# A quarter of the modulation sums of a two-layer diffusion block: product on GpSimd, row sum on ScalarE, bias on VectorE

## The chip, the core and the metric

The kernel runs on one core of a Trainium2 chip. A core has five engines that each run their own instruction stream in order and wait for one another through semaphores: TensorE (PE, matrix products into PSUM; PEld is its weight load), VectorE (DVE), ScalarE (ACT), GpSimd (POOL) and SyncE (SP, which here only issues loads). The metric is the device time of one launch in microseconds (us), lower is better. Times of single stages come from one execution taken by the hardware profiler.

## The reference, cut to what matters

Two layers of a transformer block work on 256 latent tokens and 256 context tokens of width 1024. Every sublayer (feedforward, mixer, feedforward) is normalised, scaled and shifted, and gated by a modulation vector that comes from a condition: `c` for the latent tokens and `c_ctx` for the context tokens.

```
mod = (jax.nn.silu(c) @ mod_w[i] + mod_b[i]).reshape(bsz, 3, 3, 1, D_MODEL)
modc = (jax.nn.silu(c_ctx) @ mod_w[i] + mod_b[i]).reshape(3, 3, D_MODEL)
...
lat = lat + 0.5 * mod[:, 0, 2] * _swiglu(_modulate(lat, norm_g[i, 0], mod[:, 0, 0], mod[:, 0, 1]), ffn_w13[i, 0], ffn_w2[i, 0])
```

`mod_w[i]` is 1024 x 9216 in float32. Its product with two vectors is the part that the change touches; nearly all other work is in the large products of feedforward, convolution and attention.

## The kernel before, in words

Activations lie transposed in SBUF: 8 tiles `x[:, m, :]` of 128 features by 512 tokens (256 latent, 256 context). Each float32 product is made of three products of float32r halves: a weight or activation is split in a high half `wh` (ScalarE, L107, a copy with rounding) and a low half `wl` (VectorE, L108, the difference), and `mm3` (L132) issues wh x mh, wh x ml and wl x mh (L136, L137, L138).

A feedforward (`ffn`, L813) goes in three thirds of the 22 hidden blocks. In each third, `Pair` objects (L696) compute gate and up projections with a Strassen-like scheme of seven products of quarter matrices: `head` (A11, A12), `five` (S1), `six` (S2, S4), `seven` (S3) and `four` (A22). A pair loads two raw tiles; GpSimd negates one half (L709) and then issues an accumulating load (L712) and another for A22's low half (L114), and VectorE forms the sums S (L731, L739). After `seven` VectorE adds (L776), reading the PSUM tile `p`, into which `four` adds its product afterwards. Then come gm = silu(gate) x up (L785) and its split into gh (ScalarE) and gl (VectorE), which the following `project` (L588) uses as its last operand tiles. `project` works on 8 output tiles; with a pair still open, its first three output tiles run interleaved with that pair's `seven` and `four`, and their last operand comes at the end. Outputs are scaled by the gate column (L563, ScalarE) and added to x by an accumulating DMA that GpSimd issues (L566), or by VectorE (L572).

The modulation of layer 0's first two chunks is made on TensorE at the start. All the rest is made as small **units** that fill VectorE: `jobs` lists tiles of 128 x 1024 weights (`modT`), one per output column tile (`kt = 2 * pair + j`, with j = 0 or 1). SyncE loads one job ahead into the ring of raw tiles `wr` (8 buffers, shared with the weights, L102) or, late in the kernel, into `wm` (L167). One unit (`mod_unit`, L171) multiplies the raw tile with the row `scbc[:, v, :]` (silu of the condition, the same in all partitions), sums along the row, scales, adds the bias and writes one column `mt[:, kt, v]`: one fused VectorE instruction over 128 x 1024 elements (L177) with a small read of the accumulator behind it. There are two units per job, v = 0 for the latent and v = 1 for the context condition; from layer 1's chunk 5 on only v = 0. `tick(n)` (L214) is called by the loops and issues n units: about one per pair (0.9), and three to four per output tile in the first five tiles of `project` (L624, L635). `mod_ready` and `gate` issue what is still missing when a column is needed.

Outside of stretches written out by hand, a scheduler sets the order on each engine from these program positions, so instructions of one engine can change places when the program changes.

Of the kernel before, what the change touches and what calls it, by code (L numbers as in the profile page):

```python
# [12 lines left out]
AF = mybir.ActivationFunctionType  # L13
ALU = mybir.AluOpType
# [34 lines left out]
def hybrid_kernel(ctx: ExitStack, tc: tile.TileContext, a: dict, out: bass.AP):  # L49
    nc = tc.nc  # L50
# [12 lines left out]
    def nm(s):  # L63
        uid[0] += 1
        return f"{s}{uid[0]}"
# [14 lines left out]
    ccol, modb, normg, ident, rowsum = (first[:, a:b] for a, b in zip(CUTS, CUTS[1:]))  # L80
    ccol = ccol.rearrange("p (k v) -> p k v", v=2)
    modb = modb.rearrange("p (l c) -> p l c", l=2)
    normg = normg.rearrange("p (l j k) -> p l j k", l=2, j=3)
    x = act.tile([P, KT, T2], F32, name="x", tag="x")
    for q in range(4):
# [7 lines left out]
        out=const.tile([P, 1], F32, name="silu", tag="silu"), in_=eps_t, func=AF.Silu  # L93
# [4 lines left out]
    scbc = mp.tile([P, 2, D], F32, name="scbc", tag="scbc", bufs=1)  # L98


    def load_raw(src, n=1024):
        raw = wp.tile([P, 1024], F32, name=nm("wr"), tag="wr", bufs=8)  # L102
        nc.sync.dma_start(raw[:, :n], src)
        return raw
# [47 lines left out]
    done = {}  # L152

    def mod_tile(l, ch):
        if (l, ch) not in modv:
            modv[l, ch] = const.tile([P, KT, 2], F32, name=f"mod{l}_{ch}", tag=f"mod{l}_{ch}")
            done[l, ch] = 0
        return modv[l, ch]
# [12 lines left out]
    def mod_unit(l, ch, pair, raw, j, v):  # L171

        mt = mod_tile(l, ch)
        kt = pair * 2 + j
        col = ch * KT + kt
        junk = mp.tile([P, D], BF16, name=nm("junk"), tag="junk", bufs=1)
        nc.vector.tensor_tensor_reduce(  # L177
            out=junk,
            in0=raw,
            in1=scbc[:, v, :],  # L180
            scale=0.5 if ch in (2, 8) else 1.0,
            scalar=modb[:, l, col : col + 1],
            op0=ALU.mult,
            op1=ALU.add,
            accum_out=mt[:, kt, v : v + 1],
        )
        done[l, ch] += 1
# [12 lines left out]
    def next_unit():  # L200
        if not units:
            l, ch, pair, j = jobs.pop(0)
            mod_tile(l, ch)
            raw = coming.pop() if coming else load_mod(l, ch, pair, j)
            if jobs:
                coming.append(load_mod(*jobs[0]))
            units.extend((l, ch, pair, raw, j, v) for v in range(streams(l, ch)))
        if place:
            with tc.issue_after(place[0]):
                mod_unit(*units.pop(0))  # L210
        else:
            mod_unit(*units.pop(0))
# [1177 lines left out]
    for kv in range(KVH):  # L1390
# [7 lines left out]
        out=scq, in0=rq[:, :16], scalar1=float(P) ** -0.5, scalar2=None, op0=ALU.mult  # L1398
# [76 lines left out]
    for i in range(2):  # L1475
        raw = [load_raw(a["wo"][i, :, c : c + 1024]) for c in (0, 1024)]
# [133 lines left out]
```

## Time and profile before

| | |
|---|---|
| median of 3 runs | 1549.41 us (1548.96 to 1549.91) |
| the profiled execution's own time | 1548.97 us |
| its span, first to last instruction | 1547.2 us |
| TensorE busy | 1533.5 us (99%) |
| VectorE busy | 1298.2 us (84%) |
| ScalarE busy | 852.2 us (55%) |
| GpSimd busy | 301.3 us (19%) |
| modulation units (L177) | 224, 269.9 + 19.2 us |

Line numbers such as L177 are those of the kernel before. In a row of a group, `out<-in` names the tiles, then come the shapes, the count, the busy time in us, the mean of one in ns, and after the second bar the idle time of the engine just before, with what ended it. A row of the timeline begins with its start in us from the span's start and its duration; brackets at its end hold the idle time before it and what ended that. In the list of waits, "A <- B" is A waiting for B.

### The profile page before, as it was taken

What the parts mean: (1) busy time and instruction counts of PE and PEld (TensorE: products, weight loads), DVE (VectorE), ACT (ScalarE), POOL (GpSimd) and SP (SyncE); (2) the same over time, 40 slices, a digit from 0 to 9 for tenths busy, and PEclk for the clock granted to TensorE, in tenths of its full rate; (3) what the DMA queues carried; (4) which work ended last, traced back from release to release, by engine and by line L of the source; (5) the groups of instructions that cost most, each with busy time, mean ns of one, the idle gap of its engine ahead of it and who ended that gap; (6) DMA issues with size and microseconds to landing.
All of it is one profiled execution on the core that took longest, in us unless ns stands there. A gap on an engine that the chain in (4) does not pass through costs nothing.

```text
span 1547.2 us, 27333 instructions
## 1 busy us (share of the span) xinstructions
PE 1533.5 (99%) x10594; PEld 1423.6 (92%) x10594; DVE 1298.2 (84%) x1964; ACT 852.2 (55%) x1468; POOL 301.3 (19%) x265
## 2 busy tenths in 40 slices
PE   8999999999999999999999999999999999999999
PEld 6898998999999899989999899989999899998888
DVE  5888788898989999968979889958968788998676
ACT  5644554645655376446456466446456456774553
POOL 0013313402231023042052112043042002300000
PEclk9999999999999999999999999999999999999999
DMA  9568768765356636695796625785697743476562
GB/s 377 199 188 235 162 184 232 164 194 143 75 143 175 206 91 151 212 216 135 213 214 153 207 68 136 220 189 138 210 220 182 253 159 114 142 246 220 170 195 76
DMA packets 97474, 278.80 MB, mean 180 GB/s; under 512 B 11456, under 2 KB 13120, under 8 KB 97344
## 3 DMA queue, kind: packets, MB, share of 16 engines
q1 hardware_dynamic: 69408, 228.10, 45.4%
q0 software_dynamic: 25920, 47.20, 18.1%
q10 hardware_dynamic: 2016, 1.76, 0.4%
q8 instruction: 83, 1.36, 0.4%
q14 instruction: 47, 0.39, 0.1%
HBM read 262.07 MB, written 1.05 MB: 170 GB/s over the span
## 4 chain that ended last, share of the span: by engine, by line
PE 89%; DVE 6%; DMA 2%; ACT 1%; issue 1%; POOL 0%; SPq 0%; DVEq 0%; POOLq 0%; ACTq 0%
PE p L138 8%; PE p L137 8%; PE p L136 8%; PE py L137 8%; PE py L136 8%; PE py L138 8%; PE q L138 6%; PE q L136 6%; PE q L137 6%; PE py L144 2%; PE pu L144 2%; PE pg L144 2%; DVE wl L108 1%; DMA wr<-in_w 1%; PE py L146 1%
## 5 line engine op out<-in xcount | busy, mean ns | idle before, releaser
L107 ACT ACTIVATE wh<-wr 128x1024 fp32r<-128x1024 f32 (+2 forms) x454 | 400.5, 909 | 289.2 <-PE py L137 94.5
L108 DVE TENSOR_TENSOR wl<-wr,wh 128x1024 fp32r<-128x1024 f32 (+2 forms) x454 | 468.6, 1056 | 107.0 <-ACT wh L107 87.0
L177 DVE CUSTOM_DVE_ANT_0 junk<-wr,scbc,first 128x1024 bf16<-128x1024 f32 x209 | 269.9, 1291 | 2.2 <-DMA wr<-in_modT 0.2
L137 PE MATMUL py<-gl,wh 128*128 128x512 f32 (+1 forms) x570 | 213.4, 374 | 0.0
L136 PE MATMUL py<-gh,wh 128*128 128x512 f32 (+1 forms) x570 | 213.4, 374 | 0.0
L138 PE MATMUL py<-gh,wl 128*128 128x512 f32 (+1 forms) x570 | 212.8, 373 | 0.0
L709 POOL TENSOR_SCALAR wr<-wr 128x512 f32<-128x512 f32 x66 | 125.4, 1900 | 424.0 <-DMA wr<-in_w 162.7
L136 PE MATMUL p<-th,wh 128*128 128x256 f32 x528 | 149.5, 283 | 0.0
L138 PE MATMUL p<-th,wl 128*128 128x256 f32 x528 | 149.4, 283 | 0.0
L137 PE MATMUL p<-tl,wh 128*128 128x256 f32 x528 | 149.4, 283 | 0.0
L138 PEld LDWEIGHTS py<-gh,wl 128*128 128x128 f32 x570 | 107.3, 188 | 19.1
L136 PEld LDWEIGHTS py<-gh,wh 128*128 128x128 f32 x570 | 107.4, 188 | 18.3
L137 PEld LDWEIGHTS py<-gl,wh 128*128 128x128 f32 x570 | 107.4, 188 | 18.2
L138 PE MATMUL q<-bh,wl 128*128 128x256 f32 x400 | 113.2, 283 | 0.0
L137 PE MATMUL q<-bl,wh 128*128 128x256 f32 x400 | 113.2, 283 | 0.0
L136 PE MATMUL q<-bh,wh 128*128 128x256 f32 x400 | 113.2, 283 | 0.0
L136 PEld LDWEIGHTS p<-th,wh 128*128 128x128 f32 x528 | 101.3, 192 | 0.4
L137 PEld LDWEIGHTS p<-tl,wh 128*128 128x128 f32 x528 | 101.3, 192 | 0.4
L138 PEld LDWEIGHTS p<-th,wl 128*128 128x128 f32 x528 | 101.3, 192 | 0.0
L114 POOL DMA_DIRECT2D w4l<-in_w x56 | 53.2, 949 | 229.9 <-ACT w4l L113 183.5
L566 POOL DMA_DIRECT2D x<-yg x48 | 44.7, 995 | 215.7 <-ACT yg L563 172.4
L772 ACT ACTIVATE sg<-sg 128x512 f32<-128x512 f32 x56 | 35.3, 631 | 89.0 <-DVE sg L768 88.9
(321 smaller groups left out, 4199.4 us busy)
## 6 DMA issues: line engine op xcount, KB each, us to landing
wr<-in_w SPq DMA_DIRECT2D x120, 512.0 KB, 4.8
wr<-in_modT SPq DMA_DIRECT2D x113, 512.0 KB, 5.1
wr<-in_w2b SPq DMA_DIRECT2D x64, 448.0 KB, 4.0
wr<-in_w2a SPq DMA_DIRECT2D x32, 512.0 KB, 4.4
wr<-in_w SPq DMA_DIRECT2D x56, 256.0 KB, 4.6
wr<-in_w POOLq DMA_DIRECT2D x56, 256.0 KB, 6.0
w4l<-in_w POOLq DMA_DIRECT2D x56, 256.0 KB, 5.8
x<-yg POOLq DMA_DIRECT2D x48, 256.0 KB, 7.6
```

The costliest lines, as they stand in the source:

```text
L107: nc.scalar.activation(out=hi, in_=src, func=AF.Copy)
L108: return nc.vector.tensor_tensor(out=lo, in0=src, in1=hi.bitcast(F32), op=ALU.subtract)
L114: nc.gpsimd.dma_start(out=lo, in_=src, accum_op=ALU.add)
L136: nc.tensor.matmul(ps, wh, mh, start=first, stop=False, **kw)
L137: nc.tensor.matmul(ps, wh, ml, start=False, stop=False, **kw)
L138: return nc.tensor.matmul(ps, wl, mh, start=False, stop=last, **kw).ins
L144: nc.tensor.matmul(ps, w[0], m[2], start=first and n == 0, stop=False)
L146: nc.tensor.matmul(ps[:, :S], w[1], m[0], start=False, stop=last and n == len(ms) - 1)
L177: nc.vector.tensor_tensor_reduce(out=junk, in0=raw, in1=scbc[:, v, :], scale=0.5 if ch in (2, 8) else 1.0, scalar=modb[:, l, col : col + 1 ...
L566: nc.gpsimd.dma_start(out=x[:, m, :], in_=t, accum_op=ALU.add)
L709: nc.gpsimd.tensor_scalar(out=r1[:, :T2], in0=r2[:, :T2], scalar1=-1.0, scalar2=None, op0=ALU.mult)
L772: nc.scalar.activation(out=self.sg, in_=self.sg, func=AF.Silu)
```

## The change

For units with v = 1 and j = 1, the fused VectorE instruction is replaced by three instructions on three engines. GpSimd multiplies the raw tile by `scbc[:, 1, :]` in place. ScalarE copies the tile onto itself with the scale (0.5 for chunks 2 and 8) and accumulates the row sum into the output column. VectorE adds the bias column to that column. The raw tile is thereby overwritten, after unit v = 0 has read it, and its buffer is free once ScalarE has read it. In layer 0, 7 chunks x 4 pairs and in layer 1, 5 chunks x 4 pairs have such a unit: 48 of 224.

```diff
         col = ch * KT + kt
+        if v == 1 and j == 1:
+            out = mt[:, kt, v : v + 1]
+            nc.gpsimd.tensor_tensor(out=raw, in0=raw, in1=scbc[:, v, :], op=ALU.mult)
+            nc.scalar.activation(
+                out=raw, in_=raw, func=AF.Copy, scale=0.5 if ch in (2, 8) else 1.0, accum_out=out
+            )
+            nc.vector.tensor_scalar(
+                out=out, in0=out, scalar1=modb[:, l, col : col + 1], scalar2=None, op0=ALU.add
+            )
+            done[l, ch] += 1
+            return
         junk = mp.tile([P, D], BF16, name=nm("junk"), tag="junk", bufs=1)
```

In the changed program SyncE's loads stand in the same order as before, and TensorE's order differs in a few places only. On VectorE, ScalarE and GpSimd the scheduler places many of the old instructions differently too.

## The prediction

> **What bounds the kernel now.** I read the busy shares on the page first, then the chain that ended last, then the list of TensorE's waits, then the stages.
>
> ```profile
> PE 1533.5 (99%) x10594; PEld 1423.6 (92%) x10594; DVE 1298.2 (84%) x1964; ACT 852.2 (55%) x1468; POOL 301.3 (19%) x265
> ...
> PE 89%; DVE 6%; DMA 2%; ACT 1%; issue 1%; POOL 0%; SPq 0%; DVEq 0%; POOLq 0%; ACTq 0%
> ```
>
> TensorE is busy for 1533.5 of 1547.2 us and carries 89% of the chain. A vector engine with less work is worth something only where TensorE waits today, and the list of its waits, without those of the opening 25 us, is short:
>
> ```profile
> PE pg L136 <- ACT bh L391: 1.4, 1, 1.4
> PE q L136 <- ACT gm L762: 1.2, 1, 1.2
> PE pg L137 <- DVE bl L108: 1.2, 3, 0.4
> PE q L138 <- DVE wl L108: 1.0, 1, 1.0
> ...
> PE ss L269 <- DVE acc L262: 0.5, 2, 0.3
> ...
> PE pt L1455 <- POOL pn L1442: 0.2, 1, 0.2
> PE psc L136 <- DVE ptl L108: 0.2, 1, 0.2
> PE pg L137 <- DVE bl L392: 0.2, 1, 0.2
> ```
>
> The columns are total us, times, longest. They add up to 5.9 us: that is all the change could win, 0.4% of the span. What it could lose is not bounded that way, so I looked at the stages where the modulation's sums crowd, against one stretch of the steady pair loop (last row):
>
> ```profile
> core 0: us, PE busy (x) PEld busy (x) DVE busy (x) ACT busy (x) POOL busy (x), PEclk, DMA share, GB/s
> 112.00:142.00 30.00, 30.00 (x145) 25.31 (x144) 28.34 (x42) 9.09 (x15) 3.80 (x5) 1.00 0.76 229
> 225.00:265.00 40.00, 40.00 (x189) 33.59 (x188) 33.77 (x54) 15.22 (x27) 11.18 (x11) 1.00 0.83 235
> ...
> 981.00:1006.00 25.00, 25.00 (x135) 21.62 (x134) 24.65 (x39) 8.57 (x15) 2.20 (x4) 1.00 0.73 230
> 1099.00:1115.00 16.00, 16.00 (x83) 13.70 (x82) 15.76 (x28) 3.52 (x6) 0.00 (x0) 1.00 0.65 218
> 160.00:205.00 45.00, 45.00 (x377) 45.00 (x377) 36.64 (x49) 26.76 (x46) 14.14 (x12) 1.00 0.73 165
> ```
>
> In these project stages VectorE is busy 84 to 99% of the time, ScalarE 22 to 38%, GpSimd 0 to 28%. TensorE never stops in them. So the stage is tight on VectorE, with work prepared a few us ahead of TensorE, and the question is what a longer relay through three engines does to those few us.
>
> **The change part by part.** Its condition holds for the second vector (v = 1) of odd tiles (j = 1): 7 chunks x 4 pairs in layer 0 and 5 x 4 in layer 1, so 48 of the 209 + 15 = 224 sums.
>
> ```profile
> L108 DVE TENSOR_TENSOR wl<-wr,wh 128x1024 fp32r<-128x1024 f32 x250 | 307.9, 1241 | 60.9 <-ACT wh L107 46.7 <-ACT sg L676 9.5 <-PE pu L146 3.1
> L177 DVE CUSTOM_DVE_ANT_0 junk<-wr,scbc,first 128x1024 bf16<-128x1024 f32 x209 | 269.9, 1291 | 2.2 <-DMA wr<-in_modT 0.2
> ...
> L177 DVE CUSTOM_DVE_ANT_0 junk<-wm,scbc,first 128x1024 bf16<-128x1024 f32 x15 | 19.2, 1282 | 2.2 <-DMA wm<-in_modT 2.2
> L177 DVE DVE_READ_ACCUMULATOR2_ANT mod<- 128x1 f32 x224 | 18.8, 84 | 0.0
> ...
> L1420 DVE TENSOR_SCALAR nb<-mx,scq 128x1 f32<-128x1 f32 x16 | 3.4, 214 | 0.5
> ```
>
> Removed on VectorE: 48 x (1.291 + 0.084) = 66 us. Added there: 48 additions of one column, at most 0.214 us each by the two-operation row, 10 us. Net 56 us less.
>
> ```profile
> L107 ACT ACTIVATE wh<-wr 128x1024 fp32r<-128x1024 f32 x250 | 263.3, 1059 | 200.8 <-DVE wr L731 67.7 <-PE py L137 52.5 <-PE p L137 29.9
> ...
> L1431 ACT ACTIVATION_READ_ACCUMULATOR e<-psc,nb,scq 128x1 f32 x16 | 3.1, 194 | 0.0
> ```
>
> Added on ScalarE: 48 x (1.059 + 0.194) = 60 us; its share goes from 55 to 59%. It is a copy, which the kernel already uses between all other functions, so I add no table load.
>
> Added on GpSimd: 48 products of 128x1024 with two inputs. No such instruction is in the trace. The nearest row has half the elements and one input:
>
> ```profile
> L709 POOL TENSOR_SCALAR wr<-wr x66: 1481/1830/3990, 73.7 to 1179.4; 128x512 f32<-128x512 f32 x66
> ```
>
> ```profile
> L709 POOL TENSOR_SCALAR wr<-wr 128x512 f32<-128x512 f32 x66 | 125.4, 1900 | 424.0 <-DMA wr<-in_w 162.7 <-DVE wl L108 115.0 <-ACT wh L107 35.4
> ```
>
> The first row gives minimum, median and maximum, the second the mean, 1900 ns. Below, one product cannot beat 1.5 us (min of a half-sized one). Above, four times that, 5.9 us, if elements and inputs both double it. I take twice the minimum, 2.96, plus what the row's mean stands above its minimum, 0.42: about **X = 3.5 us**. [...]
>
> The two engines also get in each other's way:
>
> ```profile
> 1020.37 1.84 POOL L709 TENSOR_SCALAR wr<-wr 128x512 f32<-128x512 f32 x1
> ```
>
> ```profile
> 1020.38 2.02 DVE L108 TENSOR_TENSOR wl<-wr,wh 128x1024 fp32r<-128x1024 f32 x1 [0.53 <-ACT wh L107]
> ```
>
> The split beside it took 2.02 us where its group (first row of VectorE's list above) has a mean of 1.24, and GpSimd took 1.84 instead of 1.48. [...] Here a delay is seen, but of 0.8 us, not of the whole 1.84.
>
> What decides is the **relay**. Before, the second sum follows the first on VectorE at once. Now: first sum (VectorE), product (GpSimd, in place, so it must wait for the first sum), row sum (ScalarE), addition (VectorE). From the end of the first sum to the addition pass X + 1.25 + about 0.15 = 4.9 us. Both ScalarE and VectorE run in order, so what stands behind the row sum or the addition waits too. The instruction order of the changed program puts only 1.3 to 4.6 us of VectorE work between the first sum and its addition at 29 of the 48 places, all in project stages. Two of these stages, worked through.
>
> Stage at 225 us. Before:
>
> ```profile
> 218.88 0.33 SPq L103 DMA_DIRECT2D wr<-in_modT  x1
> ```
>
> ```profile
> 228.13 1.28 DVE L177 CUSTOM_DVE_ANT_0 junk<-wr,scbc,first 128x1024 bf16<-128x1024 f32 x1
> ...
> 229.55 0.43 DVE L776 TENSOR_TENSOR p<-p,gm 128x256 f32<-128x256 f32 x1
> ...
> 234.63 0.68 DVE L785 TENSOR_TENSOR gm<-sg,p 128x512 f32<-128x512 f32 x1
> ...
> 236.44 0.69 DVE L108 TENSOR_TENSOR gl<-gm,gh 128x512 fp32r<-128x512 f32 x1
> ```
>
> ```profile
> 232.78 0.28 PE L136 MATMUL p<-th,w4h 128*128 128x256 f32 x1
> ...
> 239.91 0.39 PE L137 MATMUL py<-gl,wh 128*128 128x512 f32 x1
> ```
>
> ```profile
> wr<-in_modT SPq DMA_DIRECT2D x113, 512.0 KB, 5.1
> ```
>
> L776 reads p, and TensorE may add the product four to p only afterwards: 229.98 against 232.78, 2.8 us to spare. The last pair's gl must stand at 239.9; it stood at 237.1, 2.8 to spare. The changed order on VectorE is, in short:
>
> ```
> first sum A | sg | wl | gm | sum | gl | ADD A | sum | first sum B | L776 p | wl | sum | ADD B | sum | first sum | gm | sum | gl
> ```
>
> Tile A lands at 218.9 + 5.1 = 224.0; first sum to 225.3; product to 228.8; row sum to 230.0; on ScalarE the last but one gh stands behind it, to 230.7; its gl to 231.4; addition 231.5; two sums to 234.1; L776 to 234.5. TensorE waits 234.5 - 232.8 = 1.7 us. Product of B 234.1 to 237.6, row sum 238.9, addition 239.0, two sums 241.6, gm 242.3, one more sum, gl 244.3, against 239.9 + 1.7: 2.7 us more. Together 4.4 us. With X = 2.4 it is 2.2, with 5.9 it is 9.2.
>
> Stage at 112 us, the same steps: first sum of its j = 1 tile to 112.9, product 116.4, row sum 117.6, addition 117.7, next first sum 119.0, wl 120.1, L776 120.4; second product 119.0 to 122.5, row sum 123.8, addition 123.9, two sums, gm 127.1, sum, gl 129.1. Today:
>
> ```profile
> 120.00 0.28 PE L136 MATMUL p<-th,w4h 128*128 128x256 f32 x1
> ...
> 127.81 0.39 PE L137 MATMUL py<-gl,wh 128*128 128x512 f32 x1
> ```
>
> TensorE waits 0.4 and then 0.9: 1.3 us; with X = 2.4 nothing, with 5.9 6.0. Seven stages hold three or more of the products (from 112, 225, 505, 637, 752, 981, 1099 us). I give six the 1.3 and one the 4.4: **+12.2**. Some ten products stand alone in the pair loop, where ScalarE idles 18 of 45 us; 0.2 us each, **+2**. The loads that wait for a released buffer (SyncE's order is unchanged) see 48 tiles about 3.4 us later and the others earlier; I cost that at nothing, since tiles in these stages wait longer than that for VectorE (A landed at 224.0 and was first read at 228.1), and count its risk in the upper end.
>
> ```profile
> 272.76 0.38 PE L136 MATMUL q<-hh,wh 128*128 128x256 f32 x1 [1.25 <-ACT gm L762]
> ...
> 552.13 0.39 PE L136 MATMUL pg<-bh,wh 128*128 128x256 f32 x1 [1.43 <-ACT bh L391]
> ```
>
> Won: these two waits lie just behind such stages, where VectorE has one or two sums less ahead; of their 2.7 us I take **-2.5**.
>
> Sum: +12.2 + 2 - 2.5 = +11.7. The profiled execution took 1548.97 us (span 1547.2 and 1.8 around it), so 1560.7; the median of the runs is 0.4 above it. I say **1561 us**.
>
> **The rivals.**
> [...]
> 2. Faster. If GpSimd takes under about 1.8 us, no stage stalls (L776 then ends before 232.8), and 3 to 5.9 us of the waits go: 1543 to 1546. For it: VectorE at 99% in two stages, now with 1.2 us less per product. Against: it needs X close to its lowest bound.
> 3. Full serialisation. If each product also stops VectorE for all of X, it takes 3.5 to 5.9 us from VectorE to give back 1.2, in stages with 1 to 16% of idle time, and seven stages lose 6 to 9 us each: 1590 to 1610. [...] Against: the mean of the 66 GpSimd products now is only 0.4 us above the minimum, with VectorE busy 84% of the time.
> 4. It does not relieve VectorE. Same traffic, lower price: net VectorE busy falls by less than 30 us of the 56. It is no time of its own: I count it, with 0.10, inside the forecast's 0.63.
>
> **How the numbers follow.** A measurement of this kernel can tell about 0.2%, 3.1 us, from no change. Forecast and its neighbours (1552.5 to 1590): 0.63. Rival 1: 0.15. Rival 2: 0.12. Rival 3: 0.10. So faster 0.12, same 0.15, slower 0.73. The range runs from 1546, where rival 1 begins, to 1595, the sum with X = 5.9 (9.2 + 6 x 6.0 + 2 - 2.5 = +45).
>
> **What would show it.** Right: products of 3 to 4 us in the profile; VectorE's waits now name the row sum (addition behind ScalarE), ScalarE's name the product; TensorE gets waits behind gl, gh and L776 in the stages listed and nowhere else; VectorE's busy time is 30 to 56 us less. Wrong: a product near 2 us with no new TensorE wait (rivals 1 and 2); splits that double beside each product (rival 3); or new TensorE waits in the pair loop, behind late loads or GpSimd's queue, which I costed at almost nothing.

## The result and the profile after

The kernel before took 1549.66 us in the runs taken beside the changed one (median of 4, 1548.96 to 1550.32), the changed kernel **1615.1 us** (median of 4, 1613.15 to 1616.11). The ratio is 1.0421, 95% interval 1.0409 to 1.0433: 65.4 us slower, above the upper end of the predicted range, 1595. In rows of the changed kernel the line numbers are 11 higher: the fused sum is L188 (was L177), L776 is L787, L785 is L796, L709 is L720. L178 is the product, L179 the row sum, L182 the addition.

The busy shares and the shares of the chain, from the page of after:

```profile
PE 1555.1 (96%) x10594; PEld 1434.2 (89%) x10594; DVE 1324.6 (82%) x1916; ACT 898.4 (56%) x1564; POOL 431.9 (27%) x313
...
PE 44%; DVE 10%; issue 3%; ACT 3%; DMA 2%; POOL 2%; DVEq 0%; SPq 0%; POOLq 0%; ACTq 0%
```

VectorE lost 48 sums and is nevertheless busy 26.4 us longer than before (1324.6 against 1298.2). The 44% of the chain are not to be set beside the 89% of before: in after the chain can be followed back only to 575.6 us, and its shares add up to 64% of the span. Of that part TensorE carries 69% (44 of 64), VectorE 16%, against 6% before. The span grew by 66.8 us (1614.0 against 1547.2). Of this 21.6 us is TensorE busy for longer with the same 10594 matmuls, and 45.2 us is TensorE idle. The list of its waits in after (total us, times, longest) names the idle time:

```profile
PE ss L280 <- DVE acc L273: 11.5, 3, 8.5
PE p L136 <- DVE p L787: 10.2, 8, 3.6
PE py L137 <- DVE gl L108: 7.6, 6, 2.4
PE p L136 <- ACT sg L767: 7.2, 3, 4.2
PE py L136 <- ACT gh L107: 4.6, 4, 1.6
PE py L138 <- DVE wl L108: 4.3, 5, 1.5
PE q L138 <- DVE wl L108: 4.1, 4, 2.5
```

Most of it is behind VectorE (acc, p, gl, wl), so I looked at what VectorE's instructions cost. First its groups in after, then one group of before that is not shown yet:

```profile
L108 DVE TENSOR_TENSOR wl<-wr,wh 128x1024 fp32r<-128x1024 f32 x250 | 321.6, 1295 | 73.9 <-ACT wh L107 60.0 <-ACT sg L687 9.5 <-PE pu L146 3.1
L188 DVE CUSTOM_DVE_ANT_0 junk<-wr,scbc,first 128x1024 bf16<-128x1024 f32 x161 | 260.8, 1620 | 2.1 <-DMA wr<-in_modT 1.0
...
L108 DVE TENSOR_TENSOR wl<-wr,wh 128x896 fp32r<-128x896 f32 x64 | 82.0, 1290 | 13.2 <-ACT wh L107 7.7 <-PE pu L146 3.1 <-ACT sg L687 2.4
```

```profile
L108 DVE TENSOR_TENSOR wl<-wr,wh 128x896 fp32r<-128x896 f32 x64 | 69.0, 1087 | 11.6 <-ACT wh L107 6.2 <-PE pu L146 3.1 <-ACT sg L676 2.4
```

The same instructions have become longer: 161 sums by 1.620 - 1.291, 250 splits by 1.295 - 1.241 and 64 splits by 1.290 - 1.087 us. That is 53.0 + 13.5 + 13.0 = 79.5 us, about 1.7 us for each of the 48 products. (Below, "held" is the time by which VectorE's instructions that overlap a product exceed the lower quartile of their group, that is, the length that the fastest quarter stays below, in the same trace. By that count it is about 86 us here, 1.8 for a product.) The product itself, as minimum, median and maximum in ns:

```profile
L178 POOL TENSOR_TENSOR wr<-wr,scbc x48: 2352/2790/3447, 78.3 to 1177.7; 128x1024 f32<-128x1024 f32 x48
```

The timeline shows how the two meet. One stretch of after, VectorE first and GpSimd second (start, duration):

```profile
126.97 0.68 DVE L796 TENSOR_TENSOR gm<-sg,p 128x512 f32<-128x512 f32 x1
127.57 3.10 DVE L188 CUSTOM_DVE_ANT_0 junk<-wr,scbc,first 128x1024 bf16<-128x1024 f32 x1
...
130.60 0.68 DVE L108 TENSOR_TENSOR gl<-gm,gh 128x512 fp32r<-128x512 f32 x1
```

```profile
127.18 2.40 POOL L178 TENSOR_TENSOR wr<-wr,scbc 128x1024 f32<-128x1024 f32 x1 [4.09 <-DMA wr<-in_modT]
```

The sum at 127.57 takes 3.10 us instead of 1.28: the product ends at 129.58, and the sum ends 1.09 us later. As it needs 1.28 us, it made almost no way until the product was over. The split gl, for which TensorE waits, came that much later. A second stretch:

```profile
175.94 1.22 DVE L108 TENSOR_TENSOR wl<-wr,wh 128x1024 fp32r<-128x1024 f32 x1
177.33 0.69 DVE L779 TENSOR_TENSOR sg<-q,sg 128x512 f32<-128x512 f32 x1 [0.17 <-issue]
178.71 0.69 DVE L796 TENSOR_TENSOR gm<-sg,p 128x512 f32<-128x512 f32 x1 [0.69 <-PE p L138]
```

```profile
176.10 3.31 POOL L178 TENSOR_TENSOR wr<-wr,scbc 128x1024 f32<-128x1024 f32 x1 [4.31 <-DVE mod L188]
```

Here the product came second. It waited for the split to end at 177.16 and took its 2.25 us from there. L779 and L796 then ran beside it at their usual 0.69: each reads one operand from PSUM (q, p) and one from SBUF. In the whole of after, 34 sums beside a product are held 55 us together, and 15 runs of L779 and L796 beside one 0.1 us. So in after product and VectorE excluded each other in both directions (the sum at 127.57 ended 1.09 us after the product, the product at 176.10 took 3.31 us), and VectorE was held where it read two operands from SBUF, not where it read one from PSUM. For GpSimd instructions with one input e7 below shows much less: there one of at least 1.48 us holds VectorE 0.2 us in the mean.

### The profile page after: what moved, and what is told of

The parts are those of the page before. It is cut to its first block, busy times and chain, and to the rows that moved or that the text cites. A ratio compares the mean times of both kernels' runs of the same rounds, so it can differ in the third digit from the quotient of the medians.

```text
span 1614.0 us, 27463 instructions
## 1 busy us (share of the span) xinstructions
PE 1555.1 (96%) x10594; PEld 1434.2 (89%) x10594; DVE 1324.6 (82%) x1916; ACT 898.4 (56%) x1564; POOL 431.9 (27%) x313
## 4 chain that ended last, share of the span: by engine, by line
PE 44%; DVE 10%; issue 3%; ACT 3%; DMA 2%; POOL 2%; DVEq 0%; SPq 0%; POOLq 0%; ACTq 0%
PE py L138 4%; PE py L137 4%; PE py L136 4%; DVE wl L108 3%; PE p L136 3%; PE p L137 3%; PE p L138 3%; DVE junk L188 3%; PE q L136 2%; PE q L138 2%; PE q L137 2%; PE py L144 2%; PE pu L144 2%; PE pg L144 2%; POOL wr L178 1%
## 5 line engine op out<-in xcount | busy, mean ns | idle before, releaser
L108 DVE TENSOR_TENSOR wl<-wr,wh 128x1024 fp32r<-128x1024 f32 (+2 forms) x454 | 497.2, 1118 | 120.1 <-ACT wh L107 100.6
L188 DVE CUSTOM_DVE_ANT_0 junk<-wr,scbc,first 128x1024 bf16<-128x1024 f32 x161 | 260.8, 1620 | 2.1 <-DMA wr<-in_modT 1.0
L720 POOL TENSOR_SCALAR wr<-wr 128x512 f32<-128x512 f32 x66 | 118.6, 1798 | 341.5 <-DVE wl L108 158.5
L178 POOL TENSOR_TENSOR wr<-wr,scbc 128x1024 f32<-128x1024 f32 x48 | 140.0, 2917 | 232.9 <-DVE mod L188 202.6
L179 ACT ACTIVATE wr<-wr 128x1024 f32<-128x1024 f32 x48 | 50.9, 1060 | 162.2 <-POOL wr L178 162.2
L750 DVE TENSOR_TENSOR wr<-wr,wr 128x1024 f32<-128x1024 f32 x66 | 80.9, 1226 | 27.4 <-ACT w4h L112 25.9
```

Source lines behind the costliest of these rows:

```text
L108: return nc.vector.tensor_tensor(out=lo, in0=src, in1=hi.bitcast(F32), op=ALU.subtract)
L178: nc.gpsimd.tensor_tensor(out=raw, in0=raw, in1=scbc[:, v, :], op=ALU.mult)
L179: nc.scalar.activation(out=raw, in_=raw, func=AF.Copy, scale=0.5 if ch in (2, 8) else 1.0, accum_out=out)
L188: nc.vector.tensor_tensor_reduce(out=junk, in0=raw, in1=scbc[:, v, :], scale=0.5 if ch in (2, 8) else 1.0, scalar=modb[:, l, col : col + 1 ...
L720: nc.gpsimd.tensor_scalar(out=r1[:, :T2], in0=r2[:, :T2], scalar1=-1.0, scalar2=None, op0=ALU.mult)
L750: tt(out=v(r2), in0=v(r2), in1=s2.unsqueeze(1).to_broadcast([P, 2, T2]), op=ALU.subtract,)
```

## The experiments

Theory **hold**: the loss is VectorE standing still beside each product. Theory **relay**: it is the chain product, row sum, addition in queues that run in order, as I had predicted. Theory **order**: it is the scheduler's new order on VectorE, ScalarE and GpSimd. ("Port" in the expectations is hold.) Each experiment is one run, and its time stands beside one run of the kernel before on the same chip (1549.92 for e1 to e4, 1550.14 for e5 to e8, 1548.99 for e9 to e11). The four runs of the kernel before above spread over 1.4 us and the four of the changed one over 3.0, so a difference of 3 us says little here.

| run | what it is | us | against before | VectorE busy |
|---|---|---|---|---|
| e1_shadow | before + 48 products that nobody reads | 1608.63 | +58.7 | 1385.4 |
| e2_fill | after, two fills for the product | 1567.03 | +17.1 | 1242.3 |
| e3_tiny | after, a fill of one column for the product | 1557.67 | +7.8 | 1244.5 |
| e4_pairs | after, only the 12 units of the pair loop | 1576.65 | +26.7 | 1292.4 |
| e5_defer | after, row sum and addition issued later | 1614.14 | +64.0 | 1320.9 |
| e6_nosum | after without the row sum | 1599.54 | +49.4 | 1328.8 |
| e7_oneinput | before + 48 pairs of one-input shadows | 1558.47 | +8.3 | 1314.8 |
| e8_shadowpairs | e1 at the 12 units of the pair loop | 1557.63 | +7.5 | 1315.9 |
| e9_halves | e1, each product as two halves | 1597.07 | +48.1 | 1372.3 |
| e10_pairsnosum | e4 without the row sum | 1553.32 | +4.3 | 1300.2 |
| e11_floor | after without product and row sum | 1547.25 | -1.7 | 1242.3 |

**e1_shadow** adds the product alone to the kernel before. The order of the instructions on the four other engines stays what it was.

```diff
+        if v == 1 and j == 1:
+            shade = mp.tile([P, D], BF16, name=nm("shade"), tag="shade", bufs=1)
+            nc.gpsimd.tensor_tensor(out=shade, in0=raw, in1=scbc[:, v, :], op=ALU.mult)
         junk = mp.tile([P, D], BF16, name=nm("junk"), tag="junk", bufs=1)
```

> The kernel before with all 224 fused sums kept on VectorE, and 48 GpSimd products added beside them: the same 128x1024 two-input product of the raw tile with the condition's row, written to a scratch tile that nobody reads. The order on TensorE, VectorE, ScalarE and SyncE is that of the kernel before. Theory port (GpSimd's reading of two SBUF inputs holds up VectorE's instructions with two SBUF inputs): VectorE's busy time rises by 70 to 100 us, TensorE stalls in the project stages, 1590 to 1640 us. Theory relay (what costs is the chain of waits GpSimd, ScalarE, VectorE): nobody waits for these products but the buffer release, 1549 to 1556 us. Theory order (the scheduler's new order costs): 1549 to 1553 us.

It lost 58.7 us, nearly the whole loss, with no relay and no new order at all. Its rows are the product, the fused sum and TensorE's longest list entry:

```profile
L178 POOL TENSOR_TENSOR shade<-wr,scbc 128x1024 bf16<-128x1024 f32 x48 | 137.9, 2873 | 264.2 <-DMA wr<-in_modT 213.3 <-ACT scbc L1090 50.4
```

```profile
L180 DVE CUSTOM_DVE_ANT_0 junk<-wr,scbc,first 128x1024 bf16<-128x1024 f32 x209 | 316.7, 1515 | 2.5 <-DMA wr<-in_modT 0.6
```

```profile
PE p L136 <- DVE p L779: 21.9, 8, 5.5
```

A result that nobody reads makes 209 sums 0.224 us longer each (1515 against 1291), and TensorE waits 21.9 us for L776 (here L779). VectorE is busy 87.2 us longer than before; the held time beside its products is about 94 us by the count above.

**e2_fill** and **e3_tiny** keep the relay and take the reading away. Their 48 columns do not hold the modulation.

```diff
-            nc.gpsimd.tensor_tensor(out=raw, in0=raw, in1=scbc[:, v, :], op=ALU.mult)
+            for _ in range(2):
+                nc.gpsimd.memset(raw, 1.0)
```

For e3 the added line is `nc.gpsimd.memset(raw[:, :1], 1.0)`.

> The changed kernel with each GpSimd product replaced by two fills of the raw tile with ones: GpSimd writes and reads nothing, so 48 modulation columns are sums of ones, not of products. The relay GpSimd, ScalarE, VectorE stays as it is, with the fills taking some 1.5 to 3 us. Theory port: no contention, VectorE's busy time falls by 50 us or more against before, 1545 to 1556 us. Theory relay: the same waits as in the changed kernel, 1600 to 1620 us. Theory order: 1600 us or more as well.

> The changed kernel with each GpSimd product replaced by a fill of one column of the raw tile (about 0.1 us), so 48 columns are sums of raw weights and not of products. The relay stays, its GpSimd step is nearly free. Theory port: 1544 to 1551 us. Theory relay: the relay is 2.8 us shorter, so most of the loss goes, 1548 to 1570 us. Theory order (order on VectorE and ScalarE still differs from before): 1580 us or more.

The two fills take 2.05 us together (1027 ns each), close to the bare product, and cost 17.1 us. The one-column fill costs 7.8. VectorE's sums in e2, VectorE's wait for the row sum and TensorE's longest list entry:

```profile
L189 DVE CUSTOM_DVE_ANT_0 junk<-wr,scbc,first 128x1024 bf16<-128x1024 f32 x161 | 206.3, 1281 | 6.3 <-DMA wr<-in_modT 5.3
```

```profile
DVE mod L183 <- ACT wr L180: 13.4, 13, 7.2
```

```profile
PE p L136 <- ACT sg L768: 5.7, 3, 3.0
```

The fills, which only write, did not hold VectorE: the sums are at 1281 ns, against 1291 in before. What is left of the loss is the relay, with the order that the scheduler gave it. e2's time lies between the ranges of both theories; e3's lies in that of the relay.

**e6_nosum** and **e11_floor** take the relay's end away. In e6 VectorE writes the bias column without a sum, in e11 the product is left out as well; the 48 columns lack their sums. TensorE's order is the same in both, and VectorE's differs at one place.

```diff
             nc.gpsimd.tensor_tensor(out=raw, in0=raw, in1=scbc[:, v, :], op=ALU.mult)
-            nc.scalar.activation(
-                out=raw, in_=raw, func=AF.Copy, scale=0.5 if ch in (2, 8) else 1.0, accum_out=out
-            )
             nc.vector.tensor_scalar(
-                out=out, in0=out, scalar1=modb[:, l, col : col + 1], scalar2=None, op0=ALU.add
+                out=out, in0=modb[:, l, col : col + 1], scalar1=1.0, scalar2=None, op0=ALU.mult
             )
```

> The changed kernel with the product on GpSimd, but without ScalarE's row sum: VectorE writes the bias column alone, at the same place (48 columns lack their sum). Nothing waits for the product but the next load into the buffer. Hold theory: VectorE's busy time stays above 1300 us and the time is 1590 to 1610. Relay theory: without ScalarE in the chain the time is 1549 to 1560.

> The changed kernel with neither product nor row sum: the 48 columns get the bias alone (their sums are left out). What relieving VectorE of 48 sums is worth when nothing takes their place: TensorE's waits of 5.9 us after the opening are the most that can go, so 1543 to 1549. Against e6, which has the product besides, it gives the price of the hold with VectorE relieved: 1599.5 less this, about 50 us by the hold theory.

Both came out as the hold theory said. The four kernels make a ladder with the same relief on VectorE, each step taken against before: e11 -1.7; with the product 49.4, so the **hold costs 51.1 us**; with the row sum as well 65.4, so **the relay costs 16.0**. By the other way round the relay with fills costs 17.1 + 1.7 = 18.8. And -1.7 is all that 48 sums less on VectorE are worth here, 0.1% and hardly more than the runs of the kernel before spread. The order on VectorE, ScalarE and GpSimd in e11 is not that of before, and it loses nothing, so a new order as such does not explain the loss. But between e6 and after the order on VectorE and ScalarE differs as well, so the 16.0 hold the relay together with that, not separated.

The two stages that the prediction worked through tell the same. The columns are the stretch, busy us of TensorE, its weight load, VectorE, ScalarE and GpSimd with counts, granted clock (the share of the full clock that TensorE was given), DMA share, GB/s. After, then e6 (product, no relay), then e2 (relay, no reading):

```profile
113.00:145.00 32.00, 28.23 (x134) 22.88 (x133) 31.70 (x38) 11.98 (x20) 17.78 (x8) 1.00 0.66 190
228.00:270.00 42.00, 37.07 (x174) 30.35 (x175) 39.36 (x50) 19.31 (x34) 19.68 (x12) 0.96 0.76 233
```

```profile
113.00:145.00 32.00, 28.66 (x135) 23.24 (x135) 31.71 (x35) 6.89 (x12) 16.88 (x8) 1.00 0.62 195
228.00:270.00 42.00, 37.50 (x170) 30.60 (x169) 38.30 (x44) 13.82 (x25) 20.92 (x13) 0.92 0.77 222
```

```profile
110.00:140.00 30.00, 30.00 (x149) 25.41 (x148) 28.87 (x47) 16.02 (x27) 13.04 (x14) 1.00 0.79 242
226.00:266.00 40.00, 40.00 (x190) 33.60 (x189) 31.07 (x50) 21.96 (x40) 23.04 (x23) 1.00 0.92 262
```

TensorE stands still 3.8 and 4.9 us in after, 3.3 and 4.5 in e6, and not at all in e2. In these stages the loss is nearly all hold: 7.8 of the 8.7 us stay without the relay.

**e4_pairs, e8_shadowpairs, e10_pairsnosum** look at the 12 units of the pair loop. e4 changes only these, e8 is e1 with the same condition, e10 is e4 with e6's edit (12 columns lack their sums).

```diff
-        if v == 1 and j == 1:
+        if v == 1 and j == 1 and place:
```

> The change made only for those 12 units that the pair loop issues; the 36 of the project stages stay fused on VectorE. Theory port: VectorE has 18% idle time there, so the 12 blocks of 1.8 us are mostly absorbed, 1549 to 1556 us. Theory relay: loss in proportion to the relays, 12 of 48 of 65 us, 1560 to 1570 us.

e4 lost 26.7 us, 2.2 for each product, more than either theory had. Only 12 us of VectorE's time is held in it. TensorE's longest list entry in e4:

```profile
PE p L136 <- ACT sg L767: 12.3, 4, 5.8
```

One of these waits in the timelines of ScalarE and GpSimd:

```profile
810.39 1.06 ACT L179 ACTIVATE wr<-wr 128x1024 f32<-128x1024 f32 x1 [6.85 <-POOL wr L178]
...
814.85 0.38 ACT L767 COPY sg<-p 128x256 f32<-128x256 f32 x1
```

```profile
807.04 0.89 POOL L723 DMA_DIRECT2D wr<-in_w  x1 [0.41 <-POOL wr L720]
807.66 2.69 POOL L178 TENSOR_TENSOR wr<-wr,scbc 128x1024 f32<-128x1024 f32 x1
```

ScalarE stood 6.85 us at the row sum, because the product stood in GpSimd's queue behind the negated half and the load that it issues. Behind the row sum 3.4 us of splits and scaled outputs were due before sg at 814.85, and TensorE stood 5.8 us. The next two runs tell whether that is the loss ("the third run" in their expectations is e4_pairs):

> The kernel before plus shadow products only at the 12 units issued in the pair loop (the same 12 that the third run changed, order on the other engines as before). That run lost 26.7 us with 12 us of extra VectorE time and ScalarE's wait for products at 42.9 us. If its loss was the relay (TensorE behind sg, which stands behind the row sum on ScalarE), this run is within 1550 to 1558. If it was the hold, it is near 1570 as well.

> The third run again (product on GpSimd only for the 12 units of the pair loop, 1576.65 us), but without ScalarE's row sum: VectorE writes the bias column alone (12 columns lack their sum). Relay theory for the pair loop (TensorE behind sg, sg behind the row sum on ScalarE): the waits behind sg go and the time is 1550 to 1560. Hold theory: it stays above 1570.

Both say relay: the same 12 products cost 7.5 us as shadows, and 4.3 without the row sum. The row sum in ScalarE's queue is 26.7 - 4.3 = 22.4 us of e4. And of the hold's 51.1 us only 4 to 8 belong to the pair loop, where VectorE has room; the other 36 products, in the crowded stages, make the rest, some 1.2 to 1.3 us each by subtraction. The 22.4 us of these 12 row sums alone are more than the 16.0 that all 48 add in after: the parts do not add up, and the order differs a little between e4 and e10 as well, so how the relay's price comes about in after is not shown. TensorE is busy 8.3 us less in e10 than in e4 (1536.1 against 1544.4), and its wait behind sg fell from 12.3 to this:

```profile
PE p L136 <- ACT sg L764: 2.0, 1, 2.0
```

**e5_defer** issues row sum and addition two fused units later in the program.

```diff
+            def rest():
                 nc.scalar.activation(
...
+            pend.append([2, rest])
             return
```

> The changed kernel, all of it computed, with the row sum on ScalarE and the addition on VectorE issued two fused units after the product, so that ScalarE's and VectorE's queues reach them when the product is done. If the loss is the relay in order (ScalarE waits 162 us for products in the changed kernel), that wait falls under 40 us and the time comes down to 1560 to 1580. If the loss is the hold of VectorE beside each product (1.78 us per product there), the wait falls as well but the time stays at 1595 to 1612, near the shadow run's 1608.6; TensorE's waits then name VectorE's gl, wl and p, and not ScalarE's sg.

The time stayed at 1614.1 us, but the run does not tell the theories apart: the scheduler put the row sums back to nearly the same places. ScalarE's wait for the product, in after and in e5:

```profile
ACT wr L179 <- POOL wr L178: 162.2, 45, 7.0
```

```profile
ACT wr L189 <- POOL wr L186: 157.5, 43, 6.8
```

So the expectation that this wait falls under 40 us failed, the time lies in neither of the two ranges, and a relay with a later row sum was not tested.

**e7_oneinput** asks whether it is GpSimd's reading as such.

```diff
+            for c in (0, 512):
+                nc.gpsimd.tensor_scalar(
+                    out=shade[:, c : c + 512], in0=raw[:, c : c + 512], scalar1=-1.0, scalar2=None, op0=ALU.mult
+                )
```

> The kernel before plus 48 shadow pairs of one-input GpSimd instructions (two halves of 512, float32 read, bfloat16 written, nobody reads the result) where the shadow run had one two-input product; the order on the four other engines is that of before. GpSimd is busy about as long (2 x 1.48 us at least against 2.35). If any GpSimd read holds VectorE for the whole instruction, VectorE loses 48 x 1.8 to 2.2 us as with the product, and the time is near 1605. If the hold goes with what the instruction reads, as in the kernel before (about 0.4 us beside one half of 512), VectorE loses 48 x 0.4 to 0.8 us, and the time is 1552 to 1568.

```profile
L179 POOL TENSOR_SCALAR shade<-wr 128x512 bf16<-128x512 f32 x96 | 173.8, 1827 | 211.8 <-DMA wr<-in_modT 211.4
```

```profile
L183 DVE CUSTOM_DVE_ANT_0 junk<-wr,scbc,first 128x1024 bf16<-128x1024 f32 x209 | 277.5, 1328 | 2.4 <-DMA wr<-in_modT 0.5
```

GpSimd is busy longer with these 96 instructions (173.8 us) than with e1's 48 products (137.9), and yet the sums only go from 1291 to 1328 ns, against 1515 there. Beside all one-input GpSimd instructions VectorE is held about 36 us, against 15 in before: 0.4 us more per pair. The time, 1558.5, lies in the range for a hold that goes with what the instruction reads. A one-input instruction here held VectorE 0.2 us of its mean length of 1.83, the two-input product of e1 about 2.0 us (94 / 48) of 2.87.

**e9_halves** is e1 with two products of 128x512.

```diff
-            nc.gpsimd.tensor_tensor(out=shade, in0=raw, in1=scbc[:, v, :], op=ALU.mult)
+            for c in (0, 512):
+                d = slice(c, c + 512)
+                nc.gpsimd.tensor_tensor(out=shade[:, d], in0=raw[:, d], in1=scbc[:, v, d], op=ALU.mult)
```

> The shadow run again (kernel before, order of the four other engines unchanged, 48 products that nobody reads), with each product made as two GpSimd instructions of 128x512. If an instruction holds VectorE only while it runs itself, VectorE gets in between the halves: no single VectorE instruction is held over 1.5 us where the shadow run shows 2.2, but the sum of the holds stays near its 93 us, and the time stays at 1595 to 1610. If the hold comes from the length of one GpSimd instruction only, the sum falls under 60 us and the time under 1590.

Two instructions of VectorE beside such halves:

```profile
236.08 2.31 DVE L182 CUSTOM_DVE_ANT_0 junk<-wr,scbc,first 128x1024 bf16<-128x1024 f32 x1
...
238.65 1.96 DVE L182 CUSTOM_DVE_ANT_0 junk<-wr,scbc,first 128x1024 bf16<-128x1024 f32 x1
```

They are held 1.0 and 0.7 us. Instructions held for more than 1.5 us went from 40 in e1 to 3 (none was expected), and those held for more than 0.5 us from 48 to 76. The sum fell from about 94 to 82 us and the loss against before by 10.6 us, to a time within the expected 1595 to 1610. VectorE does get in between, so shorter instructions help a little, but the hold goes mostly with the whole work, not with the length of one instruction.

No version here that does all of the work beats the kernel before: even e11, which leaves the work out, is only 1.7 us below it, and e3, the relay with next to no GpSimd work, is 7.8 above.

## Why the prediction was wrong

- **What bounds the kernel: right.** TensorE had 5.9 us to win and all else to lose. e11 won 1.7, and the two waits that the -2.5 counted on are gone in it.
- **The failed step: the hold of VectorE, which the sum costed at nothing.** The prediction said "The two engines also get in each other's way", saw one delay of 0.8 us "not of the whole 1.84", and let it enter only as 0.42 us in X. The row was of a one-input GpSimd instruction. In e7 those held VectorE only 0.2 us each, and the two-input product, by the timeline of after, held it to its end at 129.58. The missing term was 51.1 us. Full serialisation was rival 3, with a chance of 0.10 and 1590 to 1610; with the relay on top it went past its upper end. The argument against it, the mean of 66 GpSimd products that stood only 0.4 us above their minimum, spoke of that other kind of instruction, and of GpSimd's delay where VectorE's was asked.
- **VectorE's relief: wrong sign.** "30 to 56 us less" became 26.4 more. The parts: 66 - 10 = 56 removed as worked out (an addition took 204 ns), about 86 held. Rival 4 had a fall of less than 30 at no price of its own; the price was the main thing.
- **X: too long.** 3.5 predicted (2.96 + 0.42 is 3.38, rounded up), 2.35 measured bare, 2.92 in the mean with its own waits for VectorE. By the prediction's own steps a shorter X gives a smaller loss (2.2 us for the stage at 225 us and nothing for the one at 112 with 2.4), so this error moved the forecast towards the result by luck. No run shows the lower end of the range, 1546: the bare 2.35 us came with a loss of 65.4, and the lowest time, e11 at 1547.25, leaves the products and sums out.
- **The relay: right in size by luck, wrong in place.** +14.2 was predicted (12.2 in seven stages, 2 in the pair loop), 16.0 measured, the order included. But the stages that I worked out lose nothing to it (e2), and TensorE's waits behind L776 and gl in after, which stand where I had put them, come mostly from the hold (e6 has most of them too). The 4.4 us for the stage at 225 us, measured at 4.9, was a hit by chance. Alone, the pair loop cost 22.4 us by its row sums, not 2: I had taken ScalarE's idle time as cover, and what decided was that GpSimd's queue was late and ScalarE waits in order (6.85 us at one row sum, with sg behind it). In after the three waits behind sg are 7.2 us; how much of the 16.0 they and their followers make was not separated.
- **VectorE waits for the addition: not seen.** In after this wait is in total below 1 us; VectorE is itself too late to wait. It appears in e2 (13.4 us), where nothing holds it.
- **The signs.** Of what should have shown the prediction wrong, two came true: "splits that double" (31 of them beside products are held 29 us together) and new TensorE waits behind "GpSimd's queue" (clearest in e4). Of what should have shown it right, ScalarE's waits for the product and TensorE's waits behind gl, gh and L776 came true too, but the hold makes these waits of TensorE as well, so they could not tell the two apart.

## What to carry to other kernels

Before moving work from VectorE to GpSimd, look at what the two read: a two-input GpSimd product and a VectorE instruction with two operands in SBUF took turns here, so 140 us of products cost VectorE about 86 us to relieve it of 56. Work with an operand in PSUM passed beside it (15 instructions, held 0.1 us together), and so did work beside fills (the sums at 1281 ns). A price read from a row of another kind of instruction is no price: a shadow, the new instruction added to the old kernel with a result that nobody reads, measures it without a change of order.

## What the runs showed beyond that

TensorE also lost speed, not only time. Busy us, then granted clock, around the wait at 388.8 us in after:

```profile
380.00:388.80 8.80, 8.80 (x65) 1.00 0.77 160
388.80:391.50 2.70, 0.01 (x2) 1.00 0.84 144
392.50:395.80 3.30, 3.30 (x17) 0.50 0.21 72
396.00:400.00 4.00, 4.00 (x35) 1.00 0.00 0
```

Behind a stall of 2.7 us the clock was halved for 3.4 us. After has six such stretches of 3.4 us, each behind a stall of over 2 us, and one of 10.2 us that begins 5.0 us into the stall of 8.5; the stalls of 2.0 us at 129 and of 2.5 us at 521 have none behind them, and in e6 the clock is 0.92 from 228 to 270 us, about 6.7 us at half speed, with TensorE still for 4.5 us in all. In the seven stretches of after TensorE worked 26.8 us at half speed, which makes 13.4 of the 21.6 us by which it is busy for longer; the rest is unexplained. By these stretches a stall of 2 to 4 us could cost another 1.7 us behind it (half of 3.4): an estimate, and not for every stall, as those at 129 and 521 show. What halves the clock was not shown.
